# HGRN mixer on one Trainium2 core: decays as products of forget gates built by doubling, one group of small products per head, two weight buffers

## The chip, the cores and the metric

The kernel runs on 1 core of a Trainium2 chip. The metric is device time in microseconds (us), the median of 3 runs. The engines are named as in the profile: PE (TensorE, matrix products), PEld (its weight loads), DVE (VectorE), ACT (ScalarE), POOL (GpSimd) and SP (which issues the loads from memory). All data are float32; the large products are made of float32 numbers split into a high and a low part.

## The reference, cut to what matters

Two residual layers over 512 tokens of width 1024, each a token mixer and an MLP; the first mixer is a gated DeltaNet, the second an HGRN recurrence. The change concerns the second. With a forget gate f per token and channel, lower-bounded by lb, it computes for each of 8 heads (128 channels)

```python
def _hgrn2(y, w_in, lb, gnorm_w, w_out):
    proj = y @ w_in
    q, f, i, gate = jnp.split(proj, 4, axis=-1)
    log_forget = jnp.logaddexp(jnp.log(lb), jnp.log1p(-lb) + jax.nn.log_sigmoid(f))
    k = (1.0 - lb) * jax.nn.sigmoid(-f)
    q = jax.nn.silu(q.astype(f32))
    o = _hgrn2_chunked(heads(q), heads(k), heads(i.astype(f32)), heads(log_forget))
    ...
# S_t = diag(f_t) S_{t-1} + k_t v_t^T (k_t = 1 - f_t), o_t = S_t^T q_t
```

So the output at token t is the sum over earlier tokens j of v_j times the product of q_t, k_j and all forget gates between j and t, summed over channels. The reference works in chunks of 64 with cumulative sums of logarithms; any grouping of the tokens gives the same result.

## The kernel before

Activations stand transposed: channels on the 128 partitions, 512 tokens along a row. Every projection (`project`, L119) takes a weight tile of 256 output columns, loaded by SP into `raw`, split by ACT into its high part `whi` (L116) and by DVE into its low part `wlo` (L117), half a tile per instruction, and makes two blocks of 24 products of 128x512 each (L127, L128, L129). `raw` has two buffers. `whi` and `wlo` have two, and outside the DeltaNet heads a third one (tags `whi3`, `wlo3`), which every third tile takes (L103); the flag `two` switches the third off. Where `stream` (L132) is called with `wide=2`, it starts with two tiles used side by side, channel block by channel block.

`hgrn` (L628) runs over four pairs of heads. `hgrn_in` (L693) projects the next pair's f and q (two tiles) and its values (one tile, 96 products of 128x256, L707 to L709). `hgrn_gates` (L673) projects the output gates of the pair before (one tile). `hgrn_tables` (L713) applies sigmoid and SiLU on ACT and loads their tables. `hgrn_head` (L729) is the mixer of one head, at high priority. The program is written in this order, and a scheduling layer then sets each engine's queue by dependence and priority: the head's small operations are put between projections of the next pair.

In `hgrn_head`, POOL bounds f from below and scales it (L735), ACT takes its logarithm (L736). For pairs of neighbouring tokens, k and q are scaled by exponentials of half the second token's logarithm (L745 to L752) and multiplied in blocks of 32 tokens: `gram32` (L759) makes 16 products of 128x32 by 128x32, four blocks in each of four chunks, in one PSUM tile. DVE scans the logarithms into cumulative sums within 64 tokens (L773). Then for each doubling step s = 2, 4, 8, 16, 32 (`HLEVELS`) DVE subtracts sums at the middle of each block of 2s (L780, L781), ACT takes the exponential (L782), and DVE multiplies the first half with k and the second with q (L783, L784). For s below 32 `gram32` follows, and DVE copies the part that belongs to this step into `ad` under a mask (L787). For s = 32, eight products go to their place by ACT (L793, L796). POOL puts `ad` into the chunk's 128x128 matrix `a` (L798). The exponentials of the whole sums give `qf` and `kg` (L802 to L812), from which come the products across 64 tokens (L816), the transposed `kg` (L824), the states of the chunks (L829, L834, L836) and the output (L841, L843). A product of float32 numbers stands in the trace as two records, the split projections as one.

After the eight heads come the row norm (L188), the output projection (L854) and the MLP.

Of the kernel before, what the change touches and what calls it, by code (L numbers as in the profile page):

```python
# [11 lines left out]
F32 = mybir.dt.float32  # L12
# [3 lines left out]
ALU = mybir.AluOpType  # L16
# [17 lines left out]
class Net:  # L34
# [44 lines left out]
    def after(self, i, prev):  # L79
        self.tc.add_manual_dep(  # L80
            i.ins, prev.ins.name,
            mybir.DependencyInfo(mybir.DependencyClass.NoSync, mybir.DependencyReason.DATA),
            reason="table order")
# [148 lines left out]
    def setup(self, w):  # L232
# [29 lines left out]
        self.lmask = self.mask("lmask", [P, len(LEVELS), B])  # L262
        self.dmask = self.const("dmask", [P, B])
# [364 lines left out]
    def hgrn(self):  # L628
# [17 lines left out]
        self.on = [None] * NH  # L646
        blocks = self.stream(a["hgrn_fq"], self.y, wide=2)
# [10 lines left out]
        for p in range(NH // 2):  # L658
# [11 lines left out]
            pr = nxt  # L670
        self.hgrn_split(range(3, NH))
# [41 lines left out]
    def hgrn_tables(self, pr, gates=()):  # L713
# [13 lines left out]
        self.table("natural_log_exp_and_others")  # L727

    def hgrn_head(self, h, kq, g, vt):  # L729
# [8 lines left out]
        tmp = lambda: self.work("ol", bufs=NH)  # L738
        gram = lambda: self.mix("gr", tag="mb")


        half = tmp()
        hv = half.rearrange("p (a n) -> p a n", a=2)
        gp = g.rearrange("p (n b) -> p n b", b=2)
        self.act(hv[:, 0], gp[:, :, 1], AF.Exp, scale=0.5)  # L745
        self.act(hv[:, 1], gp[:, :, 1], AF.Exp, scale=-0.5)
        dk, dq = tmp(), tmp()
        for dst, src, sg in ((dk, k, 0), (dq, q, 1)):
            d2, s2 = (t.rearrange("p (n b) -> p n b", b=2) for t in (dst, src))
            for b in (0, 1):  # L750
                e = nc.vector
                e.tensor_tensor(out=d2[:, :, b], in0=s2[:, :, b], in1=hv[:, (b + sg) % 2], op=ALU.mult)  # L752
        a = self.work("x" if h % 2 else "e")
        c4 = lambda t: t.rearrange("p (c t) -> p c t", c=NC)
        nc.gpsimd.memset(a, 0.0)
        blk = [slice(b, b + B) for b in range(0, P, B)]
        ad = self.work("wd" if h % 2 else "ud", [P, NC, B])

        def gram32(x, y):  # L759
            pa = self.mix("gr", [P, NC, B], tag="mb")  # L760
            for c in range(NC):
                for b in blk:
                    mm(pa[b, c], lhsT=ck(x, c)[:, b], rhs=ck(y, c)[:, b], start=True, stop=True,  # L763
                       tile_position=(0, b.start))
            return pa

        pa = gram32(dk, dq)
        nc.vector.tensor_tensor(out=ad, in0=pa, in1=self.dmask.unsqueeze(1).to_broadcast([P, NC, B]), op=ALU.mult)


        gc = g
        b64 = lambda t: t.rearrange("p (n s) -> p n s", s=64)
        nc.vector.tensor_tensor_scan(out=gc, data0=self.fresh, data1=g, initial=0.0, op0=ALU.mult, op1=ALU.add)  # L773

        for i, s in enumerate(HLEVELS):
            nb = T // (2 * s)
            v4 = lambda t: t.rearrange("p (n a s) -> p n a s", a=2, s=s)
            e = tmp()
            ref = v4(gc)[:, :, 0, s - 1:s].to_broadcast([P, nb, s])
            nc.vector.tensor_tensor(out=v4(e)[:, :, 0], in0=ref, in1=v4(gc)[:, :, 0], op=ALU.subtract)  # L780
            nc.vector.tensor_tensor(out=v4(e)[:, :, 1], in0=v4(gc)[:, :, 1], in1=ref, op=ALU.subtract)  # L781
            self.act(e, e, AF.Exp)  # L782
            nc.vector.tensor_tensor(out=v4(e)[:, :, 0], in0=v4(e)[:, :, 0], in1=v4(k)[:, :, 0], op=ALU.mult)  # L783
            nc.vector.tensor_tensor(out=v4(e)[:, :, 1], in0=v4(e)[:, :, 1], in1=v4(q)[:, :, 1], op=ALU.mult)  # L784
            if s < B:
                pa = gram32(e, e)
                nc.vector.copy_predicated(out=ad, mask=self.lmask[:, i + 1].unsqueeze(1).to_broadcast([P, NC, B]),  # L787
                                          data=pa)
                continue
            pa = self.mix("gr", [P, NC, B], tag="mb")  # L790
            for c in range(NC):
                for l, r in (blk[0:2], blk[2:4]):
                    mm(pa[l, c], lhsT=ck(e, c)[:, l], rhs=ck(e, c)[:, r], start=True, stop=True,  # L793
                       tile_position=(0, l.start))
            for l, r in (blk[0:2], blk[2:4]):
                nc.scalar.copy(out=c4(a)[l, :, r], in_=pa[l])  # L796
        for b in blk:
            nc.gpsimd.tensor_copy(out=c4(a)[b, :, b], in_=ad[b])  # L798


        qf, kg = tmp(), tmp()
        self.act(qf, gc, AF.Exp)  # L802
        last = self.work("last", [P, 2 * NC], bufs=2)
        egl = self.work("egl", [P, NC], bufs=2)
        nc.vector.tensor_copy(out=last, in_=b64(qf)[:, :, 63])
        lv = last.rearrange("p (c b) -> p c b", b=2)
        nc.vector.tensor_tensor(out=egl, in0=lv[:, :, 0], in1=lv[:, :, 1], op=ALU.mult)
        nc.vector.tensor_tensor(out=qf, in0=qf, in1=q, op=ALU.mult)
        nc.vector.tensor_tensor(out=b64(kg), in0=b64(gc)[:, :, 63:64].to_broadcast([P, 2 * NC, 64]), in1=b64(gc),
                                op=ALU.subtract)  # L810
        self.act(kg, kg, AF.Exp)
        nc.vector.tensor_tensor(out=kg, in0=kg, in1=k, op=ALU.mult)  # L812
        pa = gram()
        for c in range(NC):
            t = c * P
            mm(pa[0:64, t + 64:t + P], lhsT=kg[:, t:t + 64], rhs=qf[:, t + 64:t + P], start=True, stop=True)  # L816
        nc.scalar.copy(out=c4(a)[0:64, :, 64:P], in_=c4(pa)[0:64, :, 64:P])
        for t, half, n in ((kg, slice(0, 64), NC - 1), (qf, slice(64, P), NC)):
            v = c4(t)[:, 0:n, half]
            f = lv[:, 0:n, half.start // 64 ^ 1:(half.start // 64 ^ 1) + 1]  # L820
            nc.vector.tensor_tensor(out=v, in0=v, in1=f.to_broadcast([P, n, 64]), op=ALU.mult)
# [163 lines left out]
def halves(s):  # L985

    p, t = np.arange(P)[:, None] % B, np.arange(B)[None, :]
    return (p // (2 * s) == t // (2 * s)) & (p // s % 2 == 0) & (t // s % 2 == 1)


def turned(m):
    return m.reshape(P // B, B, B).transpose(0, 2, 1).reshape(P, B)


def layout(x, gdn_w_in, gdn_conv, gdn_a_log, gdn_dt_bias, gdn_onorm, gdn_w_out, hgrn_w_in, hgrn_lb_logits,
# [10 lines left out]
    o["lmask"] = np.stack([turned(halves(1))] + [halves(s) for s in LEVELS[1:]], 1).astype(np.float32)  # L1006
    o["dmask"] = ((i[:, None] % B // 2 == i[None, :B] // 2) & (i[:, None] % B <= i[None, :B])).astype(np.float32)
# [33 lines left out]
```

## Time and profile before

| | |
|---|---|
| time, median of 3 runs | 1363.98 us (1363.65 to 1366.46) |
| the profiled execution's own time | 1365.81 us |
| its span in the trace | 1363.7 us |
| granted TensorE clock, mean | 0.996 |
| PE busy | 1338.5 us (98%), 10084 records |
| PEld busy | 1096.9 us (80%) |
| DVE busy | 823.2 us (60%), 1472 instructions |
| ACT busy | 579.3 us (42%), 1061 instructions, 37 table loads |
| POOL busy | 206.1 us (15%), 212 instructions |
| DMA | 121.5 MB, mean 89 GB/s |

The DeltaNet mixer lies at about 40 to 330 us, its output projection and the first MLP reach to about 700, the HGRN mixer fills some 720 to 965, and its output projection and the second MLP the rest. In a timeline row stand the start, the duration, engine, source line, operation, what is written and read, the shape and how many are merged; in brackets how long the engine had been idle and what ended that. Matmuls overlap, so their durations add up to more than their time: what one costs PE is read from the starts of the instructions around it.

### The profile page before, as it was taken

What the parts mean: (1) busy time and instruction counts of PE and PEld (TensorE: products, weight loads), DVE (VectorE), ACT (ScalarE), POOL (GpSimd) and SP (SyncE); (2) the same over time, 40 slices, a digit from 0 to 9 for tenths busy, and PEclk for the clock granted to TensorE, in tenths of its full rate; (3) what the DMA queues carried; (4) which work ended last, traced back from release to release, by engine and by line L of the source; (5) the groups of instructions that cost most, each with busy time, mean ns of one, the idle gap of its engine ahead of it and who ended that gap; (6) DMA issues with size and microseconds to landing.
All of it is one profiled execution on the core that took longest, in us unless ns stands there. A gap on an engine that the chain in (4) does not pass through costs nothing.

```text
span 1363.7 us, 23897 instructions
## 1 busy us (share of the span) xinstructions
PE 1338.5 (98%) x10084; PEld 1096.9 (80%) x10084; DVE 823.2 (60%) x1472; ACT 579.3 (42%) x1061; POOL 206.1 (15%) x212
## 2 busy tenths in 40 slices
PE   7999999999999999999999999999999999999997
PEld 5777777778888888888888788787888888888897
DVE  5886777766844444444483985769774444445453
ACT  5664655444344323132134566476434413314242
POOL 4001011000200120201121123031100021120232
PEclk8999999999999999999999999999999999999999
DMA  6131110222322222232220212121042223232232
GB/s 199 35 122 36 60 63 33 80 78 67 141 103 93 93 93 93 95 114 96 98 93 31 94 64 94 62 94 63 32 154 93 93 93 97 95 115 95 93 134 83
DMA packets 23498, 121.53 MB, mean 89 GB/s; under 512 B 3808, under 2 KB 7008, under 8 KB 9824
## 3 DMA queue, kind: packets, MB, share of 16 engines
q1 hardware_dynamic: 23392, 120.02, 25.3%
q8 instruction: 79, 1.29, 0.4%
q14 instruction: 27, 0.22, 0.1%
HBM read 117.91 MB, written 2.10 MB: 88 GB/s over the span
## 4 chain that ended last, share of the span: by engine, by line
PE 86%; DVE 6%; ACT 5%; issue 2%; DMA 0%; POOL 0%; SPq 0%; POOLq 0%; ACTq 0%; DVEq 0%
PE pj L127 25%; PE pj L128 25%; PE pj L129 24%; ACT L93 1%; PE gr L763 1%; PE pga L478 1%; PE pu L523 1%; ACT whi L116 1%; DVE wlo L117 1%; ACT v L87 1%; PE px L516 1%; PE pw L593 1%; PE pj L709 1%; PE pj L708 1%; PE pj L707 1%
## 5 line engine op out<-in xcount | busy, mean ns | idle before, releaser
L117 DVE TENSOR_TENSOR wlo<-raw,whi 128x1024 fp32r<-128x1024 f32 (+2 forms) x217 | 290.1, 1351 | 167.4 <-ACT whi L116 165.1
L116 ACT CAST whi<-raw 128x1024 fp32r<-128x1024 f32 (+2 forms) x222 | 221.6, 1024 | 398.5 <-PE pj L128 381.8
L127 PE MATMUL pj<-yh,whi 128*128 128x512 f32 x960 | 383.6, 400 | 0.7 <-ACT whi L116 0.7
L129 PE MATMUL pj<-yh,wlo 128*128 128x512 f32 x960 | 382.3, 399 | 0.6 <-DVE wlo L117 0.6
L128 PE MATMUL pj<-yl,whi 128*128 128x512 f32 x960 | 382.1, 398 | 0.0
L127 PEld LDWEIGHTS pj<-yh,whi 128*128 128x128 f32 x960 | 181.7, 189 | 37.4 <-ACT whi L116 1.9
L129 PEld LDWEIGHTS pj<-yh,wlo 128*128 128x128 f32 x960 | 181.7, 189 | 36.6 <-DVE wlo L117 1.0
L128 PEld LDWEIGHTS pj<-yl,whi 128*128 128x128 f32 x960 | 182.0, 190 | 35.4
L128 PE MATMUL pj<-ol,whi 128*128 128x512 f32 x336 | 131.3, 391 | 0.0
L901 DVE TENSOR_TENSOR gate<-pj,rB 128x512 f32<-128x512 f32 x56 | 38.6, 691 | 148.2 <-PE pj L129 148.2
L129 PE MATMUL pj<-oh,wlo 128*128 128x512 f32 x320 | 125.0, 391 | 0.0
L127 PE MATMUL pj<-oh,whi 128*128 128x512 f32 x320 | 124.9, 391 | 0.0
L903 POOL TENSOR_TENSOR kd<-kd,gate 128x512 f32<-128x512 f32 x18 | 23.3, 1292 | 462.2 <-DVE gate L901 458.0
L887 ACT ACTIVATE z<-pj 128x512 f32<-128x512 f32 x64 | 38.0, 594 | 113.6 <-PE pj L129 109.6
L128 PEld LDWEIGHTS pj<-ol,whi 128*128 128x128 f32 x336 | 63.2, 188 | 12.9
L127 PEld LDWEIGHTS pj<-oh,whi 128*128 128x128 f32 x320 | 60.1, 188 | 12.3
L129 PEld LDWEIGHTS pj<-oh,wlo 128*128 128x128 f32 x320 | 60.0, 188 | 12.3
L129 PE MATMUL pj<-kq,wlo 128*128 128x512 f32 (+1 forms) x192 | 68.4, 356 | 0.5 <-DVE wlo L117 0.5
L128 PE MATMUL pj<-kq,whi 128*128 128x512 f32 (+1 forms) x192 | 68.4, 356 | 0.0
L127 PE MATMUL pj<-kq,whi 128*128 128x512 f32 (+1 forms) x192 | 68.0, 356 | 0.0
L167 POOL TENSOR_TENSOR sqacc<-sqacc,z 128x512 f32<-128x512 f32 x25 | 37.3, 1494 | 122.9 <-ACT z L165 118.8
L93 ACT ACT_TABLE_LOAD x37 | 47.5, 1283 | 1.4 <-PEq L1033 0.7
(392 smaller groups left out, 2022.2 us busy)
## 6 DMA issues: line engine op xcount, KB each, us to landing
raw<-down SPq DMA_DIRECT2D x36, 1024.0 KB, 4.8
raw<-up SPq DMA_DIRECT2D x32, 1024.0 KB, 4.8
raw<-gdn_in SPq DMA_DIRECT2D x14, 1024.0 KB, 4.8
raw<-hgrn_fq SPq DMA_DIRECT2D x8, 1024.0 KB, 4.8
raw<-gdn_out SPq DMA_DIRECT2D x4, 1024.0 KB, 5.7
raw<-hgrn_i SPq DMA_DIRECT2D x4, 1024.0 KB, 4.7
raw<-hgrn_gate SPq DMA_DIRECT2D x4, 1024.0 KB, 4.8
raw<-hgrn_out SPq DMA_DIRECT2D x4, 1024.0 KB, 4.8
```

The costliest lines, as they stand in the source:

```text
L87: i = self.nc.scalar.activation(out=out, in_=in_, func=func, **kw)
L93: i = self.nc.scalar.preload_act_table_set(name)
L116: self.nc.scalar.copy(out=hi[:, k], in_=raw[:, k])
L117: eng.tensor_tensor(out=lo[:, k], in0=raw[:, k], in1=hi[:, k].bitcast(F32), op=ALU.subtract)
L127: mm(o, lhsT=hi[:, k, c], rhs=yh, start=(k == 0), stop=False)
L128: mm(o, lhsT=hi[:, k, c], rhs=yl, start=False, stop=False)
L129: mm(o, lhsT=lo[:, k, c], rhs=yh, start=False, stop=(k == NB - 1))
L167: e.tensor_tensor(out=self.sq, in0=self.sq, in1=t, op=ALU.add)
L478: mm(pga[:, c - c2], lhsT=ck(k, c), rhs=kq[:, :, c * P:(c + 1) * P], start=True, stop=True)
L887: nc.scalar.activation(out=z, in_=out, func=AF.Relu)
L901: nc.vector.tensor_tensor(out=t, in0=out, in1=self.r2b, op=ALU.mult)
L903: e.tensor_tensor(out=self.h[c], in0=self.h[c], in1=t, op=ALU.add)
```

## The change

It is in `hgrn_head` and around it.

- The decays are products of forget gates instead of exponentials of sums of logarithms. ACT makes `upto` = f scaled and bounded by lb in one instruction, POOL sets `behind` to one. `upto` holds for each token the product of gates from the start of its block to it, `behind` the product from behind it to its block's end. From blocks of s to blocks of 2s, one DVE product multiplies `behind` of the first halves by the second halves' total, and one `upto` of the second halves by the first halves' total, in place. Before each of these steps one DVE product writes both operands of the step: `behind` times k in the first halves, `upto` times q in the second. `qf` and `kg` are two products at the end. The logarithm, the scan, all exponentials and POOL's bounding and scaling are gone. ACT, not POOL, copies `ad` to its place.
- Step s = 1 has products of its own: k with q (masked to the diagonal) and k with q times f. So there are seven groups per head instead of six: six of 16 products and one of 8. All are issued behind the last DVE product of the chain: the first waits for it (the new argument `kind` of `after`), the others are ordered behind the first. They go to two PSUM tiles and are then copied under masks one after the other.
- `upto` and `behind` (four rows of 512) and `qf` and `kg` (four more) lie in the third weight buffer, so the HGRN stage works with two. `a` is cleared once per buffer instead of once per head. The products across 64 tokens use all 128 columns of `kg`.
- The table of logarithms and exponentials is loaded once behind the heads instead of after each pair. The mask `dmask` and its load are gone, `lmask` has one row more.

The diff, cut to its core:

```diff
-    def after(self, i, prev):
+    def after(self, i, prev, kind=mybir.DependencyClass.NoSync):
...
         self.on = [None] * NH
+        self.two = True
         blocks = self.stream(a["hgrn_fq"], self.y, wide=2)
...
-        self.fresh = self.work("rB", bufs=2)
-        nc.gpsimd.memset(self.fresh, 1.0)
-        nc.gpsimd.memset(self.fresh.rearrange("p (n s) -> p n s", s=64)[:, :, 0:1], 0.0)
+        xa, xb = (self.wp.tile([P, 2, 2, T], F32, tag=t, bufs=1, name=self.name(t)) for t in ("whi3", "wlo3"))
+        self.ba = [xa[:, i] for i in (0, 1)]
+        self.fg = [(xb[:, i, 0], xb[:, i, 1]) for i in (0, 1)]
+        self.hat = [self.work(t) for t in ("e", "x")]
+        for t in self.hat:
+            nc.gpsimd.memset(t, 0.0)
...
+        self.nw_tiles, self.two = 0, False
+        self.table("natural_log_exp_and_others")
         self.hgrn_split(range(3, NH))
...
-        nc.gpsimd.tensor_scalar(out=g, in0=g, scalar1=1e-37, scalar2=self.oml[:, hs], op0=ALU.max, op1=ALU.mult)
-        self.act(g, g, AF.Ln, bias=self.lb[:, hs])
+        tmp = lambda: self.work("ol", bufs=NH)
+        mul = lambda o, x, y: nc.vector.tensor_tensor(out=o, in0=x, in1=y, op=ALU.mult)
+        ba, (qf, kg) = self.ba[h % 2], self.fg[h % 2]
+        behind, upto = ba[:, 0], ba[:, 1]
+        nc.scalar.activation(out=upto, in_=f, func=AF.Identity, scale=self.oml[:, hs], bias=self.lb[:, hs])
         nc.scalar.activation(out=q, in_=q, func=AF.Copy, scale=self.oml[:, hs])
...
+        nc.gpsimd.memset(behind, 1.0)
...
+        qa = tmp()
+        mul(qa, upto, q)
+        parts = [(k, q), (k, qa)]
+        for s in (1,) + HLEVELS:
+            v4 = lambda t: t.rearrange("p (n a s) -> p n a s", a=2, s=s)
+            if s > 1:
+                e = tmp()
+                mul(e.rearrange("p (n a s) -> p n a s", a=2, s=s), halves(ba, s), halves(kq, s))
+                parts.append((e, e))
+            for t, i in ((behind, 0), (upto, 1)):
+                end = v4(upto)[:, :, 1 - i, s - 1:s].to_broadcast([P, T // (2 * s), s])
+                mul(v4(t)[:, :, i], v4(t)[:, :, i], end)
...
+        mul(kg, behind, k)
+        last = mul(qf, upto, q)
...
+        pa = [self.mix("gr", [P, n, NC, B], tag="mb") for n in (4, 3)]
+        lead = None
+        for i, (x, y) in enumerate(parts):
+            o = pa[i // 4][:, i % 4]
+            wide = i == len(parts) - 1
             for c in range(NC):
...
+                for l, r in ((blk[0:2], blk[2:4]) if wide else zip(blk, blk)):
+                    m = mm(o[l, c], lhsT=ck(x, c)[:, l], rhs=ck(y, c)[:, r], start=True, stop=True,
+                           tile_position=(0, l.start))
+                    if lead is None:
+                        lead = m
+                        self.after(m, last, mybir.DependencyClass.Sync)
+                    else:
+                        self.after(m, lead)
...
-            nc.gpsimd.tensor_copy(out=c4(a)[b, :, b], in_=ad[b])
+            nc.scalar.copy(out=c4(a)[b, :, b], in_=ad[b])
...
-            mm(pa[0:64, t + 64:t + P], lhsT=kg[:, t:t + 64], rhs=qf[:, t + 64:t + P], start=True, stop=True)
+            mm(pa[:, t + 64:t + P], lhsT=kg[:, t:t + P], rhs=qf[:, t + 64:t + P], start=True, stop=True)
```

In the program as scheduled, the small products of a head stand elsewhere on PE's queue. Here is the queue of before among the first head's products: `gr` are the small products' PSUM tiles, `ol` their operands, `pj` the projections of the next pair.

```order
L127 MATMUL pj_7061<-yh_6595,whi_7054 128x512
L763 MATMUL gr_7326<-ol_7320 32x32 x16
L128 MATMUL pj_7061<-yl_6596,whi_7054 128x512
L763 MATMUL gr_7350<-ol_7344 32x32 x16
L129 MATMUL pj_7061<-yh_6595,wlo_7055 128x512
L127 MATMUL pj_7061<-yh_6638,whi_7054 128x512
L128 MATMUL pj_7061<-yl_6639,whi_7054 128x512
L129 MATMUL pj_7061<-yh_6638,wlo_7055 128x512
L127 MATMUL pj_7061<-yh_6673,whi_7054 128x512
L128 MATMUL pj_7061<-yl_6674,whi_7054 128x512
L763 MATMUL gr_7374<-ol_7368 32x32 x16
```

After, the same head's products on PE (`wlo_1057_6915` is the third weight buffer, which now holds `kg` and `qf`; L808 are the products across 64 tokens):

```order
L126 MATMUL pj_7087<-yl_6715,whi_7054 128x512
L786 MATMUL gr_7320<-kq_6920 32x32 x16
L786 MATMUL gr_7320<-ol_7289,kq_6920 32x32 x16
L786 MATMUL gr_7320<-ol_7293 32x32 x16
L786 MATMUL gr_7320<-ol_7297 32x32 x16
L786 MATMUL gr_7321<-ol_7301 32x32 x16
L786 MATMUL gr_7321<-ol_7305 32x32 x16
L786 MATMUL gr_7321<-ol_7309 32x32 x8
L808 MATMUL gr_7438<-wlo_1057_6915 128x64 x4
L127 MATMUL pj_7087<-yh_6714,wlo_7055 128x512
```

The 104 products of the head stand together and the products across 64 tokens directly behind them; before, 46 runs hold the 48 groups of the eight heads, now there are 8 runs.

The second place is where the first two tiles of the stage end and the first values are projected. Before, on PE (`whi_6787` is the second tile, `whi_1062_6928` the value tile in the third buffer):

```order
L128 MATMUL pj_6797<-yl_6752,whi_6787 128x512
L129 MATMUL pj_6797<-yh_6751,wlo_6788 128x512
L707 MATMUL pj_6936<-whi_1062_6928,yh_6508 128x256
L708 MATMUL pj_6936<-wlo_1063_6929,yh_6508 128x256
L709 MATMUL pj_6936<-whi_1062_6928,yl_6509 128x256
```

After, at the same place (`whi_6929` and `wlo_6930` are the value tile, now in a buffer that the first tile held before):

```order
L126 MATMUL pj_6795<-yl_6750,whi_6785 128x512
L127 MATMUL pj_6795<-yh_6749,wlo_6786 128x512
L710 MATMUL pj_6937<-whi_6929,yh_6506 128x256
L710 MATMUL pj_6963<-whi_6929,yh_6506 128x256
L710 MATMUL pj_6989<-whi_6929,yh_6506 128x256
L711 MATMUL pj_6937<-wlo_6930,yh_6506 128x256
L712 MATMUL pj_6937<-whi_6929,yl_6507 128x256
```

Three products that need only the high part are drawn forward, ahead of the first that needs the low part. The DeltaNet stage, whose code is the same, is scheduled in a slightly different order as well: among other places, the block of 16 products for its decays (`pab`) stands three projections earlier at the start.

More of the change, by code (lines that the diff above doesn't have):

```diff
@@ L261, in setup @@
         nc.sync.dma_start(out=self.tri, in_=self.a["tri"])
-        self.lmask = self.mask("lmask", [P, len(LEVELS), B])
-        self.dmask = self.const("dmask", [P, B])
+        self.lmask = self.mask("lmask", [P, len(LEVELS) + 1, B])
         self.ident32 = self.const("ident32", [P, B])
@@ L745, in hgrn_head @@
[L745 to L753, printed above, removed]
@@ L771, in hgrn_head @@
[L771 to L796, printed above, removed]
@@ L797, in hgrn_head @@
-        for b in blk:
-            nc.gpsimd.tensor_copy(out=c4(a)[b, :, b], in_=ad[b])
[L801 to L808, printed above, removed]
@@ new lines, in hgrn_head @@
+        nc.vector.tensor_tensor(out=ad, in0=pa[0][:, 0], in1=self.ident32.unsqueeze(1).to_broadcast([P, NC, B]),
+                                op=ALU.mult)
+        for i in range(1, len(parts) - 1):
+            m = (len(LEVELS), 1, 2, 3, 4)[i - 1]
+            nc.vector.copy_predicated(out=ad, mask=self.lmask[:, m].unsqueeze(1).to_broadcast([P, NC, B]),
+                                      data=pa[i // 4][:, i % 4])
+        for l, r in (blk[0:2], blk[2:4]):
+            nc.scalar.copy(out=c4(a)[l, :, r], in_=pa[1][l, 2])
```

43 lines of the change are left out of this document (16 added, 27 removed).

## The prediction

> **What bounds the kernel now.** I read four views in this order: the busy times by stretch, what TensorE waited for, the groups of its instructions, and the timeline around one head. The stretches are 40 to 330 us (the DeltaNet mixer) and 722 to 965 us (the HGRN mixer, nearly the only code that is edited); columns are the stretch, its length, then busy us (instructions) of PE, PEld, DVE, ACT and POOL, the granted clock, DMA share and GB/s:
>
> ```profile
> 40.00:330.00 290.00, 284.36 (x3694) 223.70 (x3692) 218.55 (x555) 158.59 (x434) 30.82 (x57) 1.00 0.20 67
> 722.00:965.00 243.00, 239.89 (x2644) 196.48 (x2643) 174.49 (x390) 147.00 (x240) 49.39 (x52) 1.00 0.21 74
> ```
>
> In the HGRN stretch PE is busy 239.89 of 243.00 us at full clock. DVE has 68 us free there, ACT 96. So work taken from DVE, ACT or POOL is worth nothing by itself; only what shortens PE's own row of work, or its idle 3.11 us, counts. The waits of PE from 725 to 965 us (us in total, times, longest) account for nearly all of that idle time, and each is a small product waiting for its DVE operand:
>
> ```profile
> PE gr L763 <- DVE ol L784: 1.7, 5, 0.5
> PE gr L793 <- DVE ol L784: 0.7, 1, 0.7
> PE gr L763 <- DVE ol L752: 0.3, 1, 0.3
> PE po L843 <- DVE s L834: 0.2, 1, 0.2
> ```
>
> That is 2.9 us; the first three rows make seven waits of 2.7 us, 0.39 us on average.
>
> **The small products: what grouping them saves.** The groups of PE's instructions from 740 to 960 us show how many there are (each product stands as two records, so x32 in a timeline row is 16 products):
>
> ```profile
> L763 PE MATMUL gr<-ol 128*32 128x32 f32 x1024 | 14.6, 198 | 1.7 <-DVE ol L784 1.7
> ...
> L763 PE MATMUL gr<-ol,ol 128*32 128x32 f32 x256 | 3.7, 199 | 0.4 <-DVE ol L752 0.3
> L793 PE MATMUL gr<-ol 128*32 128x32 f32 x128 | 3.6, 198 | 0.7 <-DVE ol L784 0.7
> ```
>
> 1280 records at L763 are 40 groups of 16 products, 128 at L793 are 8 groups of 8: five and one per head. Busy times of matmuls overlap, so I cost a group by starts. One group of each kind stands here among projections:
>
> ```profile
> 759.74 0.39 PE L127 MATMUL pj<-yh,whi 128*128 128x512 f32 x1
> 760.05 0.46 PE L763 MATMUL gr<-ol 128*32 128x32 f32 x32
> 760.44 0.50 PE L128 MATMUL pj<-yl,whi 128*128 128x512 f32 x1
> 760.87 0.45 PE L793 MATMUL gr<-ol 128*32 128x32 f32 x16
> 761.25 0.50 PE L129 MATMUL pj<-yh,wlo 128*128 128x512 f32 x1
> 761.58 0.39 PE L127 MATMUL pj<-yh,whi 128*128 128x512 f32 x1
> ...
> 762.49 0.39 PE L128 MATMUL pj<-yl,whi 128*128 128x512 f32 x1
> ```
>
> Undisturbed, projections start 0.227 us apart (761.58 to 762.49 in four steps). From 759.74 to 761.58 pass 1.84 us with three of them; the two groups cost 1.84 - 0.68 = 1.16, so 0.58 us each. Once two groups stand in a row:
>
> ```profile
> 885.24 0.39 PE L127 MATMUL pj<-yh,whi 128*128 128x512 f32 x1
> 885.56 0.82 PE L763 MATMUL gr<-ol 128*32 128x32 f32 x64
> 886.31 0.50 PE L128 MATMUL pj<-yl,whi 128*128 128x512 f32 x1
> 886.65 0.39 PE L129 MATMUL pj<-yh,wlo 128*128 128x512 f32 x1
> ```
>
> 1.41 us less two projections is 0.95, so the second group costs 0.37: about 0.2 us of an isolated group's price is spent on going from projections to small products and back. The order of before has 46 runs for its 48 groups: 46 x 0.58 + 2 x 0.37 = 27.4 us. After, each head has one run of seven groups (one more than before, since the first doubling step needs its own products): 8 x (0.58 + 6 x 0.37) = 22.4. **Gain 5.0 us**; 0.37 rests on a single pair of groups.
>
> The order of after puts the cross products (L816 before) straight behind that run. Alone they cost:
>
> ```profile
> 763.62 0.39 PE L127 MATMUL pj<-yh,whi 128*128 128x512 f32 x1
> 763.94 0.68 PE L816 MATMUL gr<-ol,ol 128*64 128x64 f32 x8
> 764.55 0.50 PE L128 MATMUL pj<-yl,whi 128*128 128x512 f32 x1
> 764.88 0.39 PE L129 MATMUL pj<-yh,wlo 128*128 128x512 f32 x1
> ```
>
> 1.26 - 0.45 = 0.81 us, of which 0.61 lies between their own start and the next projection's. If the run shares its way in and out with them, 0.2 us a head go: **gain 1.6 us**, at worst 0 (they now use 128 weight columns instead of 64, which no row shows for 64 moving ones). I take 1.6, since they are neighbours in the order without a projection between.
>
> **Waits of PE.** The 2.9 us of waits above end with the separate groups. In their place each head's first product waits for one DVE instruction, the last product of the decay chain; queued behind it on PE's queue are the rest of the run and all projections. Eight waits at the mean of the seven seen, 0.39 us: **3.1 us** back. Ends: 0 (DVE is early) and about 1 us each, 8 us. That the two are near each other shows in the sum from the first head's run to the second's. PE has there 52 projections (11.8 us), 10 of the narrow value projections at 0.11 (rows below; 1.1) and the run with the cross products (0.58 + 6 x 0.37 + 0.61 = 3.4): 16.3 us, and the state's and the output's products besides. What DVE has there is worked out from its issue steps in this profile:
>
> ```profile
> 749.11 1.22 DVE L773 TENSOR_TENSOR_SCAN v<-rB,v 128x512 f32<-128x512 f32 x1
> 750.24 1.20 DVE L117 TENSOR_TENSOR wlo<-raw,whi 128x1024 fp32r<-128x1024 f32 x1
> 751.36 0.29 DVE L768 TENSOR_TENSOR ud<-gr,dmask 128x128 f32<-128x128 f32 x1
> 751.56 0.42 DVE L780 TENSOR_TENSOR ol<-v 128x256 f32<-128x256 f32 x1
> 751.89 0.42 DVE L781 TENSOR_TENSOR ol<-v 128x256 f32<-128x256 f32 x1
> ...
> 760.22 0.69 DVE L809 TENSOR_TENSOR ol<-v 128x512 f32<-128x512 f32 x1
> 760.82 0.30 DVE L787 COPY_PREDICATED ud<-lmask,gr 128x128 f32<-128x128 uint8 x1
> ```
>
> A product over half a head takes a step of 0.33, over a whole head 0.60, a masked step 0.20, the scan 1.13, half a weight split 1.12. The chain after is 12 half products (4.0), 8 whole ones (4.8), six small masked steps (1.2): 10.0 us. Before, 24 half products, the scan, three whole products and five masked steps made 7.9 + 1.1 + 1.8 + 1.0 = 11.8. With one weight split (2.2), two projections' scalings (1.2) and the first head's two cross scalings and three state steps (five instructions of half size or less, under 1.7), DVE has some 15 us between the two runs, and a wait of its own for the first run's products. PE's 16.3 and more just cover it, so I expect waits of tenths of a microsecond. ACT's exponentials and logarithm, POOL's floor-and-scale (L735) and the reloads of tables go; nothing of PE waited for them in the list above, so I cost that at nothing; its cover is the projections queued between a pair's heads.
>
> **Two weight buffers.** A tile lasts PE some 11 us (48 x 0.227), while its split takes ACT 2.1 us and DVE 2.4 (two halves, rows below), so two buffers do in mid-stage. They do not at one place: the stage begins with two tiles used side by side, and the third tile had its own buffer. Now its split starts when the first tile is released. The row for such a release is here, beside the stage's first value projections, with DVE's next rows:
>
> ```profile
> 737.56 1.05 ACT L116 CAST whi<-raw 128x1024 fp32r<-128x1024 f32 x1 [13.50 <-PE pj L128]
> ...
> 738.47 0.69 DVE L699 TENSOR_TENSOR kq<-pj,rB 128x512 f32<-128x512 f32 x1
> 739.08 1.22 DVE L117 TENSOR_TENSOR wlo<-raw,whi 128x1024 fp32r<-128x1024 f32 x1
> ...
> 738.95 0.28 PE L707 MATMUL pj<-whi,yh 128*128 128x256 f32 x1
> 739.06 0.28 PE L708 MATMUL pj<-wlo,yh 128*128 128x256 f32 x1
> ```
>
> The high half is then there in time for 738.95, the low half at 739.08 + 1.22 = 740.30. PE has three narrow products (0.33) that do without it: a new wait of 740.30 - 739.28 = **1.0 us** (ends 0 and 2.5, the latter if the second halves wait too).
>
> **The rest.** The order of the DeltaNet stage changes a little as well: one load of a mask goes, and a block of 16 products stands three projections earlier. PE idles 5.64 us there in all; I count 0, with 1.5 us either way.
>
> **Sum.** -5.0 - 1.6 - 2.9 + 3.1 + 1.0 = -5.4 us. The profiled execution took 1365.81 us (span 1363.7, so 2.1 around it); it would take 1360.4. It lies 1.8 above the median of the timed runs, 1363.98, so I forecast 1358.6.
>
> **Rivals.** Less than 0.2% (2.7 us) cannot be told from no change here.
>
> (a) Waits eat the gain. At 0.9 us a head: -9.5 + 1.0 + 7.2 = -1.3, 1362.7: the same. For it: DVE fills whole stretches while two heads follow each other. Against: the mean of 0.39. Chance 0.18.
>
> (b) Slower, by DVE's one long chain. It needs over 1.4 us a head (-9.5 + 1.0 + 8 x 1.4 = +2.7); at 2 us it is +7.5, 1371.5. The mechanism is seen once: POOL adds squares while DVE works, and PE waits.
>
> ```profile
> 951.56 1.28 POOL L167 TENSOR_TENSOR sqacc<-sqacc,z 128x512 f32<-128x512 f32 x1 [12.16 <-ACT z L165]
> ...
> 951.80 1.32 DVE L781 TENSOR_TENSOR ol<-v 128x256 f32<-128x256 f32 x1
> ...
> 954.91 0.45 PE L793 MATMUL gr<-ol 128*32 128x32 f32 x16 [0.75 <-DVE ol L784]
> ```
>
> The DVE product took 1.32 instead of 0.42 us and ended with POOL's. One such hit of 0.9 in each chain, on top of 0.39, gives 1.3 a head: not quite enough, and L735's work on POOL is gone. Chance 0.07. The Trainium skill ("SBUF — State Buffer", SBUF: two separate sides) states the rule: a DVE operation with two SBUF inputs and a GpSimd operation that reads SBUF lock each other out for a whole instruction. The trace agrees at 951.80; by the rule every product of the new chain is exposed, but the memsets on POOL are not readers.
>
> (c) Slower, because a long run of small products does not keep its rate. If each of the seven groups costs 0.58, a head has 4.06 + 0.61 instead of 3.43 + 0.81: +3.4 for eight, and +3.4 - 2.9 + 3.1 + 1.0 = +4.6, 1368.6. Against: the pair at 885.56. Chance 0.05. The Trainium skill ("TensorE: Matmul & The Clock Gate", Wait — 56ns, not 53.3ns?) gives a floor of about 25 ns from start to start, however small the product. Taken per record, 208 of them would be an estimated 5.2 us a head by that page; 64 records in 0.95 us are 15 ns each, so it can hold only per product.
>
> (d) More than forecast: no waits at the runs, 1363.98 - 9.5 + 1.0 = 1355.5. Chance 0.2, against 0.5 for the forecast. That the grouping isn't there is excluded by the order.
>
> **Range and chances.** Faster is the forecast and (d): 0.70. Same 0.18, slower 0.12. Low end: (d) less 1.5 for the DeltaNet order, 1354.0. High end: waits of 0.9, the cross products' 1.6 not gained, and half of the DeltaNet order's 1.5: -1.3 + 1.6 + 0.8 = +1.1, 1365.1, which holds (a).
>
> **What would show it.** Right: eight runs of 208 small records in PE's timeline, each about 2.6 us, then cross products with 0.6; PE waits at L786 of 2 to 5 us in all; one wait of 1 us at L711 near the stage's start; the stage some 5 us shorter. Wrong: run lengths over 3.5 us; waits at L786 above 1 us each; waits on whi or wlo at other places; or a change outside 722 to 965 us larger than that within.

## The result and the profile after

The changed kernel took 1379.1 us (median of 4 runs, 1377.35 to 1383.52) beside 1364.29 of the kernel before (4 runs, 1363.65 to 1366.46): 1.0111 times as long, interval 1.0084 to 1.0137. The forecast was 1358.6, at most 1365.1: the kernel became slower where faster was forecast. The profiled execution took 1378.38 us, 12.57 more than the one of before.

The two stretches that the prediction began with, in the changed kernel (same columns):

```profile
40.00:330.00 290.00, 284.51 (x3693) 224.76 (x3691) 218.06 (x551) 157.86 (x431) 32.49 (x57) 0.99 0.19 66
722.00:965.00 243.00, 225.83 (x2844) 196.77 (x2844) 166.99 (x332) 112.78 (x192) 12.16 (x12) 0.97 0.20 66
```

In the HGRN stretch PE is now idle for 17.2 us instead of 3.1, and its clock was granted at 0.97 instead of 1.00. To see the whole stage whatever its order, I take from the timelines the time between the first row-sum product of the norm ahead of it (719.1 before, 719.2 after) and that of the next norm (1047.5 and 1059.7): 328.4 us before, 340.6 after. So **12.2 of the 12.57 us are lost in this stage**. What PE waited for there, from 725 to 1065 us:

```profile
PE gr L786 <- issue: 12.8, 6, 2.4
PE gr L786 <- DVE wlo L739: 1.9, 3, 0.9
PE pj L711 <- DVE wlo L115: 0.8, 1, 0.8
PE pj L711 <- issue: 0.7, 1, 0.7
PE pt L816 <- DVE wlo L739: 0.6, 1, 0.6
PE pj L127 <- DVE wlo L115: 0.5, 1, 0.5
PE ps L821 <- ACT ol L818: 0.3, 1, 0.3
```

The waits that the prediction argued about are there in about the forecast size: 1.9 us at L786 with 0.6 and 0.3 at the transposes and states behind it, where 3.1 was forecast, and 0.8 at L711, where 1.0 was. The large row is another: 12.8 us in six pieces at the small products, ended by "issue", that is by no engine and no transfer that this list can name; 0.7 more stands at L711. The timeline has one of them in the middle of the second head's run:

```profile
784.38 0.28 PE L710 MATMUL pj<-whi,yh 128*128 128x256 f32 x1
784.59 0.46 PE L786 MATMUL gr<-kq 128*32 128x32 f32 x32
784.87 0.46 PE L786 MATMUL gr<-ol,kq 128*32 128x32 f32 x30
...
785.17 0.96 PE L786 MATMUL gr<-ol 128*32 128x32 f32 x92
788.03 0.73 PE L786 MATMUL gr<-ol 128*32 128x32 f32 x50 [1.89 <-issue]
788.69 1.10 PE L808 MATMUL gr<-wlo 128*128 128x64 f32 x8
789.60 0.36 PE L711 MATMUL pj<-wlo,yh 128*128 128x256 f32 x1
```

158 records pass in 1.36 us, then PE stands for 1.9 us between two products of one group, and the last 50 follow at the same rate. The run takes 4.1 us; "over 3.5 us" was the prediction's first sign of being wrong.

Behind some of these stops the clock falls. Busy times by stretch, around the first and the sixth head's run:

```profile
764.00:768.00 4.00, 2.18 (x40) 1.89 (x27) 1.91 (x7) 0.53 (x2) 0.00 (x0) 1.00 0.02 4
768.00:771.50 3.50, 3.50 (x13) 2.83 (x11) 2.15 (x5) 3.39 (x9) 0.00 (x0) 0.51 0.00 0
873.90:877.30 3.40, 1.00 (x103) 0.89 (x93) 2.74 (x5) 1.95 (x3) 0.00 (x0) 1.00 0.31 46
877.40:884.10 6.70, 6.70 (x33) 5.95 (x26) 2.08 (x8) 2.43 (x8) 0.00 (x0) 0.50 0.33 139
```

After a stretch in which PE did little, it runs at half clock for 3.4 or 6.8 us. The stage has three such stretches (768.10, 877.33, 945.59), 13.65 us in all; before it had none.

**What the stops have in common.** PE's weight loads, products and semaphore instructions, numbered in order of start, place the stops of the changed kernel so:

```
stop after (us)   length   instruction   modulo 256
102.17            2.27      1729         193    (DeltaNet stage)
764.07            2.01     11969         193    head 1
785.94            2.09     12481         193    head 2
806.71            0.96     13249         193    head 3, behind the run
824.78            2.18     13761         193    head 4
855.00            2.44     14529         193    head 5
874.13            2.59     15041         193    head 6
941.76            2.61     16577         193    head 8
```

A length runs from the start of the last instruction ahead of the stop to the start of the next one, so it is 0.2 to 0.3 us more than the idle time of the list. All stops stand at the same place of a period of 256. Transfers have that period too. The page of the changed kernel lists them by queue:

```profile
q8 instruction: 81, 1.33, 0.4%
```

81 packets of 16 KB for PE's 20,761 instructions, 256 in each. In the stop at 785.94, one such packet runs from 785.68 to 786.61, and PE goes on 1.4 us after it ends. The stage's other stops are alike. In all seven a packet starts 0.8 to 1.3 us after PE enters the block ahead of the stop (784.84 here), takes 0.9 to 1.4 us, and PE goes on 1.3 to 1.6 us after its end. Hence **theory F (fetch)**: PE's instructions come in blocks of 256; entering one block starts the fetch of the next, which in these stops can be used 3.2 to 3.8 us later (784.84 to 788.03 here). A projection is two instructions in 0.227 us, so a block of projections lasts 29 us; small products are 8.6 ns a record with its weight load (1.36 us by 158), so a block of them lasts 1.1 us. A run of 416 instructions drains what is there and then waits. The Trainium skill ("Runtime: NRT & Kernel Launch", Instruction fetch mechanics) also has blocks of 256 instructions, fetched one ahead. It says that the crossing is mostly hidden because instructions are dispatched more slowly than blocks are filled; here it isn't hidden, and the measurement decides.

The trace of before had such a stop, also at instruction 1729. It is among the "5.64 us there in all" that the prediction put aside:

```profile
102.90 0.59 PE L523 MATMUL pu<-ud,xd 32*32 32x32 f32 x44
104.79 0.38 PE L523 MATMUL pu<-ud,xd 32*32 32x32 f32 x20 [1.30 <-issue]
```

At this stop the packet starts late: in the kernel before 2.4 us after PE enters the block ahead of the stop, in the changed kernel 3.4. PE again goes on 1.4 and 1.6 us after the packet's end, so the next block is usable only after 5.1 and 5.9 us. The time from block to block is therefore not fixed; what holds the packet up there stays open.

The rivals: **theory W (data)**, the stops are waits for late DVE products or for PSUM that the profile can't name; **theory C (clock)**, small products in number lower the clock by themselves, and the stops are not what does it.

### The profile page after: what moved, and what is told of

It is laid out like the page before. It is cut to its first block, busy times and chain, and to the rows that moved or that the text cites. A ratio compares the mean times of both kernels' runs of the same rounds, so it can differ in the third digit from the quotient of the medians.

```text
span 1376.6 us, 24205 instructions
## 1 busy us (share of the span) xinstructions
PE 1337.1 (97%) x10340; PEld 1108.8 (81%) x10340; DVE 818.0 (59%) x1416; ACT 548.2 (40%) x1016; POOL 170.7 (12%) x172
## 3 DMA queue, kind: packets, MB, share of 16 engines
q8 instruction: 81, 1.33, 0.4%
## 4 chain that ended last, share of the span: by engine, by line
PE 85%; DVE 8%; ACT 3%; issue 2%; DMA 1%; POOL 0%; SPq 0%; POOLq 0%; ACTq 0%; DVEq 0%
PE pj L126 24%; PE pj L125 24%; PE pj L127 24%; DVE whi L739 1%; DVE ol L739 1%; PE gr L786 1%; DVE wlo L115 1%; PE pga L475 1%; DVE kq L393 1%; PE pw L590 1%; PE pu L520 1%; PE gr L808 1%; PE px L513 1%; ACT whi L114 0%; PE po L602 0%
## 5 line engine op out<-in xcount | busy, mean ns | idle before, releaser
L125 PEld LDWEIGHTS pj<-oh,whi 128*128 128x128 f32 x320 | 60.2, 188 | 12.2
L127 PEld LDWEIGHTS pj<-oh,wlo 128*128 128x128 f32 x320 | 60.0, 188 | 12.2
L739 DVE TENSOR_TENSOR whi<-whi 128x256 f32<-128x256 f32 x96 | 40.5, 423 | 7.7 <-ACT whi L742 5.8
```

What stands on the lines that cost most here:

```text
L125: mm(o, lhsT=hi[:, k, c], rhs=yh, start=(k == 0), stop=False)
L127: mm(o, lhsT=lo[:, k, c], rhs=yh, start=False, stop=(k == NB - 1))
L739: mul = lambda o, x, y: nc.vector.tensor_tensor(out=o, in0=x, in1=y, op=ALU.mult)
```

## Experiments on the stops

Each stands against runs of the kernel before on the same chip; stage lengths are from the profiled executions, measured as above (before 328.4, after 340.6).

**Operands ready early (early).**

```diff
             wide = i == len(parts) - 1
+            x, y = k, q
```

> The changed kernel, but all seven groups of a run read k and q (ready long before), so the decay chain's products are left out of the result; each run's first product still waits for the end of the chain. F: runs of 416 instructions run dry as before: 5 to 8 idle stretches of about 2 us within the runs, 9 to 17 us in all. W: with the operands long there, no idle stretch within a run: 0 to 2 us in all.

1376.02 us in one execution, stage 339.1. PE's waits from 700 us on begin with

```profile
PE gr L787 <- issue: 12.3, 6, 2.3
PE gr L787 <- DVE wlo L739: 1.9, 3, 0.9
```

The stops stay, in the same number and about the same size, each at 193 modulo 256. W is ruled out as far as operands go.

**128 instructions ahead (phase128).**

```diff
             nc.tensor.matmul(warm, lhsT=zeros[:, 0:P], rhs=zeros[:, 0:WARM], start=True, stop=True)
+        for _ in range(32):
+            nc.tensor.matmul(warm[:, 0:16], lhsT=zeros[:, 0:P], rhs=zeros[:, 0:16], start=True, stop=True)
```

> The changed kernel with 32 tiny products (128 instructions) added at the start, while PE waits for its first weights: all later PE instructions move by 128 places in the stream, nothing else moves. F, with 3.3 us from block to block: idle stretches in the HGRN stage of 2.2 us in heads 1, 3 and 7, 0.9 in head 8, 0.7 in head 5, under 0.5 in heads 2, 4 and 6: 9.0 us in all instead of 13.5; the one of 2.1 us at 102 us in the DeltaNet stage goes; 1368 to 1374 by what the clock does. W and C: the same six heads stall at the same products for the same 13 us, within 1 us of 1378.

1371.22 us, 1.0031 times before (1.0019 to 1.0043); stage 334.0. Its waits:

```profile
PE gr L788 <- issue: 6.7, 3, 2.5
PE gr L788 <- DVE wlo L741: 1.9, 3, 0.9
PE pt L818 <- DVE wlo L741: 1.9, 4, 0.7
PE pj L125 <- issue: 1.2, 1, 1.2
```

The three long stops are in heads 1, 3 and 7, as the model had them, again at 193 modulo 256; the DeltaNet stage's is gone. The model's small ones (0.7 and 0.9) did not show, and one of 1.2 stands behind head 6's run instead: 7.9 us in all, 9.0 expected. The second head's run, with the same products and operands, now goes through:

```profile
785.52 0.46 PE L788 MATMUL gr<-kq 128*32 128x32 f32 x32
785.79 0.46 PE L788 MATMUL gr<-ol,kq 128*32 128x32 f32 x30
...
786.10 1.51 PE L788 MATMUL gr<-ol 128*32 128x32 f32 x142
787.54 0.66 PE L810 MATMUL gr<-wlo 128*128 128x64 f32 x4
```

2.0 us from its start to the cross products instead of 4.1. Where a stop falls is set by the place in the instruction stream and not by the products. The kernel is otherwise the same, so data and PSUM (W) are ruled out, and a period in the stream with a 16 KB packet in each stop is what F says.

**Ungrouped (spread).**

```diff
-                    if lead is None:
-                        lead = m
-                        self.after(m, last, mybir.DependencyClass.Sync)
-                    else:
-                        self.after(m, lead)
```

> The changed kernel without the grouping: the small products of each part wait for their own DVE operand alone, and the scheduler spreads them between projections again (56 runs of 8 to 16 products instead of 8 runs of 104). Theory F (fetch): PE's instructions arrive in blocks of 256, and a block can be used about 3.3 us after PE enters the one before it; a run of 104 products is 416 instructions in about 2 us, so PE runs dry. Then here no idle time above 0.6 us between small products that no engine ends, no half-clock stretch between 700 and 1000 us; from the profiled 1378.4: -13.5 (the idle stretches) -6.8 (half of 13.6 us at half clock) +48 x 0.2 (ways in and out of runs) = 1367.7. Theory W (data): the idle stretches are waits for late DVE products or for PSUM; they stay as waits of 10 us or more, 1376 to 1380. Theory C (clock: small products by themselves lower it): idle goes only in part, half-clock stretches in the stage stay.

1371.12 us, 1.0036 times before (1.0022 to 1.005); stage 333.3, with no stop by issue and no half clock in it, though there are as many small products: C is ruled out. The time is 3.4 above F's sum. The stage has 4.0 us of idle time; the changed kernel's has 17.6, and 6.8 go to half clock. Without these, 329.3 stand against 316.2 us, so by this estimate 48 separate runs cost about 0.27 us each instead of F's 0.2.

**Two runs a head (tworuns).** The lead is the product that the rest of a run is ordered behind. A new lead stands at the fifth group; the first run's lead waits for that run's last operand.

```diff
+            if i == 4:
+                lead = None
...
-                        self.after(m, last, mybir.DependencyClass.Sync)
+                        self.after(m, (muls[4], last)[i // 4], mybir.DependencyClass.Sync)
```

> The changed kernel with each head's run cut in two, 64 products and 40, with 26 to 54 other products between. F: a run of 64 is 256 instructions, one block, and nearly every block now holds ten or more projections; at most one or two idle stretches, under 2 us in all, and no half-clock stretch in the stage. 1378.4 - 13.5 - 6.8 + 8 x 0.2 + about 1 = 1360.7, faster than both kernels. W: the products still wait for the same DVE results: 1375 to 1380. C: as many small products in each run of 3.4 us, so half-clock stretches stay: about 1368 (13.5 less idle, the rest stays).

1363.46 us, 0.9983 times before (0.9971 to 0.9995); stage 327.3. The stretch of the stage, and its first waits:

```profile
722.00:965.00 243.00, 235.09 (x2900) 202.22 (x2899) 172.39 (x344) 119.41 (x199) 13.69 (x12) 1.00 0.22 75
```

```profile
PE gr L790 <- DVE wlo L739: 4.3, 6, 1.2
PE ps L825 <- ACT ol L822: 2.6, 8, 0.4
```

The stops and the half clock are gone from the stage with one more lead a head: 13.3 us of it. The time is 2.8 us above F's 1360.7; the two rows above are 6.9 us of waits for DVE and ACT, where the changed kernel had 2.8. Its runs also give the price of grouping undisturbed:

```profile
769.01 0.40 PE L125 MATMUL pj<-yh,whi 128*128 128x512 f32 x1
769.34 0.46 PE L790 MATMUL gr<-kq 128*32 128x32 f32 x32
769.62 0.46 PE L790 MATMUL gr<-ol,kq 128*32 128x32 f32 x30
...
769.92 0.71 PE L790 MATMUL gr<-ol 128*32 128x32 f32 x62
770.57 0.50 PE L126 MATMUL pj<-yl,whi 128*128 128x512 f32 x1
```

1.56 us less one projection is 1.33 for four groups: 0.58 and three times 0.25, where the prediction had 0.37.

**Narrow cross products (narrow),** in the kernel with two runs.

```diff
-            mm(pa[:, t + 64:t + P], lhsT=kg[:, t:t + P], rhs=qf[:, t + 64:t + P], start=True, stop=True)
+            mm(pa[0:64, t + 64:t + P], lhsT=kg[:, t:t + 64], rhs=qf[:, t + 64:t + P], start=True, stop=True)
```

> The two-run kernel with the cross products as before: 64 weight columns and 64 result rows instead of 128 and 128 (only those 64 rows are read). The wide ones take 0.91 us from their start to the next projection, the narrow ones before took 0.61: if the width is the cause, 8 x 0.3 = 2.4 us less than the two-run kernel, 1361.1. If their price is only the way in and out, no change: 1363.5.

1362.0 us, 0.9978 times before (0.9968 to 0.9987). The stage goes from 327.3 to 324.9: the 2.4 expected. Each of the eight groups of cross products takes 0.61 us up to the next projection, in the two-run kernel 0.91 or 0.92. In whole times the step (0.0005) is within the intervals; up to the HGRN norm the two profiled executions already differ by 1.5 us.

**112 instructions ahead of that (narrow112),** 28 tiny products as in phase128.

> The kernel with two runs and narrow cross products, and 28 tiny products (112 instructions) at the start, while PE waits for weights. F: with 3.3 us from block to block no block boundary is then late by more than 0.1 us, also not the one at 101 us in the DeltaNet stage (2.0 us idle, and 3.4 us at half clock behind it): 2.0 + 1.7 = 3.7 us less than without the 28 products, about 1357.4, and no half-clock stretch between 40 and 1350 us. Rival: the place in the stream is nothing to PE, and it is as fast as without them, 1361, with the idle time still there.

1360.33 us, 0.996 times before (0.9948 to 0.9973); it and narrow112pool (below) are the fastest kernels here. No stop by issue and no half clock between 40 and 1349 us. From the last product of the decay inputs (`pab`) to the norm ahead of the HGRN it takes 679.26 us, narrow 683.72: 4.46 less, 3.7 expected. The profiled executions differ by 4.6 us (1357.79 and 1362.39). In whole times the gain is not shown: the five executions lie at 1357.7 (two) and 1360.4 (three), the medians differ by 1.7, and the intervals of the two ratios overlap. The longer executions may lose at the start, where narrow112pool, with the same 28 products, ends `pab` 2.9 us later; no trace shows one of them.

**A lead that waits for less (earlier), and that with 120 instructions ahead (earlier120).**

```diff
-                        self.after(m, (muls[4], last)[i // 4], mybir.DependencyClass.Sync)
+                        self.after(m, (muls[4], muls[7])[i // 4], mybir.DependencyClass.Sync)
```

> The two-run kernel with narrow cross products, and the second run's first product waiting for the last operand of its own run instead of for the very end of the decay chain, which comes four DVE instructions later. If the 4.3 us of waits for DVE in the two-run kernel are waits for that end: 2 to 3 us of them go, less 8 x 0.2 that the cross products then stand apart; 1360 to 1361. If DVE is late by more than that anyhow, they stay: 1362 to 1363.

> The kernel whose second run starts at its own last operand (1365.0), with 30 tiny products (120 instructions) at the start. F: its trace has block boundaries late by 2.6 us at 794 us and by 1.7 at 100 us, the latter with 3.4 us at half clock; by the model of 3.3 us a block no boundary is late at this place of the stream: 2.6 + 1.7 + 1.7 = 6.0 us less, about 1359. Rival (nothing hangs on the place in the stream): 1365.

1364.97 us, 1.0009 (0.9997 to 1.0021), and 1363.79, 0.9988 (0.998 to 0.9997); stages 328.9 and 327.5. The first one's wait for DVE hardly shrinks (3.9 us, now for the run's own last operand), so it was not the chain's end alone that PE waited for: a miss, and slower than either forecast. The move in the stream removes the stop of 2.6 us and the DeltaNet stage's, as F says, but only 1.2 us of the 6.0 appear in the median: at the new place PE waits 4.6 us for DVE, and the start is 4.7 us later.

**The same move elsewhere (narrowmid).** 56 tiny products of one record ahead of the first products of `gdn_decay` instead of 28 at the start.

> The kernel with two runs and narrow cross products, and 56 tiny products of one record each (112 instructions) among the first products of the DeltaNet stage instead of 28 of two records at the start, where they took 9 us of a busy start. F: the same move of 112 places in the stream, so no late block boundary and no half-clock stretch between 40 and 1350 us: the stretch from the end of the first products to the DeltaNet stage's last output product 287 us instead of 291.7, at a price of 1 us or less for the tiny products: 1362.0 - 4.0 + 1.0 = 1359. Rival (nothing hangs on the place in the stream): 1362 to 1363.

1363.69 us, 0.9991 (0.9981 to 1.0), runs from 1360.87 to 1366.37. The profiled execution is the fastest, 1360.87. It has no stop by issue over 0.3 us and no half clock between 40 and 1348 us. The stretch forecast at 287 us takes 291.7, but holds 17 projections more than in narrow (an estimated 3.9 us); up to the norm ahead of the HGRN the time from the last `pab` falls from 683.72 to 682.00, with a wait of 1.7 us at one transpose of L622 on the way. The median shows no gain over narrow: a miss. How much of a removed stop is kept depends on what is late next; that was not followed further.

## Experiments on the other terms

**Two weight buffers in the kernel before (beforetwo), and with the diagonal copies on ACT (beforetwoact).**

```diff
+        self.two = True
         blocks = self.stream(a["hgrn_fq"], self.y, wide=2)
...
-            nc.gpsimd.tensor_copy(out=c4(a)[b, :, b], in_=ad[b])
+            nc.scalar.copy(out=c4(a)[b, :, b], in_=ad[b])
```

(The last two lines in beforetwoact only. At the end of the stage both kernels set the flag back, as the changed kernel does.)

> The kernel before with nothing changed but the weight buffers of the HGRN stage: two pairs in turn instead of three. If the second buffer pair costs what the trace of the changed kernel shows (one wait of 0.7 to 0.8 us at the third tile's low half), the time is 0.5 to 1.5 us above before, hardly to be told from it. If two buffers are a main cause of the loss, 5 us or more above before.

1375.34 us, 1.0085 (1.0071 to 1.0099), 10.5 above before on this chip, which is the second case of the expectation; stage 337.2, so 8.8 longer. The wait at the third tile is 0.7 us as expected, so most of the loss is elsewhere. In its timeline, POOL's copies for the first head and the output products that read them:

```profile
760.23 8.08 POOL L800 COPY e<-ud 32x128 f32<-32x128 f32 x4 [15.88 <-DVE ud L789]
768.36 0.49 PE L843 MATMUL po<-e,uw 128*128 128x128 f32 x2 [3.85 <-POOL e L800]
```

The first of the four copies takes 7.09 us, while DVE works on without a pause; the other three take 0.28 to 0.29, and the median of the run is 0.36. Half clock follows (3.4 us).

> The kernel before with two pairs of weight buffers in the HGRN stage, and with the copies of the masked diagonal blocks on ACT instead of POOL, as the changed kernel has them. With two buffers alone it took 1375.3: one POOL copy that otherwise takes 0.3 us took 7 us while DVE ran product after product, and PE waited 3.9 us for it at the output products and then ran 3.4 us at half clock. If POOL beside DVE is the cause, ACT copies in 0.3 us and some 6 us or more go: 1366 to 1369, and what is left over before is the price of the two buffers. If the buffers themselves cost it: 1374 to 1376.

1370.19 us, 1.0034 (1.0021 to 1.0047); stage 334.3. About 5 us go with POOL's copies by the medians, less than expected, and 2.9 of the stage by the profiled executions. 5.9 of the stage stay, with waits of 0.2 to 0.9 us for DVE and ACT at many lines and 3.4 us of half clock. So in the old kernel two buffers cost more than the one wait. What they cost in the changed one can't be separated this way, since the third pair's place is in use for the products; there the trace shows 0.8, and tworuns, narrow and narrow112 are below before with two buffers.

**The copies back on POOL (narrow112pool):** the reverse of that edit, in narrow112.

> The best kernel so far (two runs a head, narrow cross products, 112 instructions ahead; 1360.3) with the diagonal copies back on POOL. If a POOL copy is held while DVE multiplies, then DVE's longer chain holds it in several heads: output products wait 1 to 4 us each, 5 to 15 us in all, 1365 to 1375. If moving the copies was worth nothing, as the prediction had it: 1360 to 1361.

1359.8 us, 0.9957 (0.9943 to 0.9971); stage 323.9 beside 324.5: the move was worth nothing here. A copy takes up to 1.37 us, and PE waits 2.2 us for them in five pieces, but 2.3 instead of 4.7 for DVE at the small products and 0.2 instead of 2.2 for ACT.

## Why the prediction was wrong, by its steps

The stage's 12.2 us, with the rows measured since: grouping 8 x (0.58 + 6 x 0.25) - 27.4 = -10.8; cross products 8 x 0.3 = +2.4; waits for DVE and ACT 2.8 - 2.9 = -0.1; the third tile +0.8; stops by issue 12.8 + 0.7 = +13.5; half clock, half of 13.65, +6.8. Sum +12.6. The stage as a whole closes in the same way: its idle time grew from 3.6 to 17.6 us, half clock cost 6.8, so the rest of PE's row became 8.6 us shorter (-10.8 + 2.4 = -8.4 by the rows).

- **The step that failed is "what grouping them saves": a run of seven groups at 0.58 + 6 x 0.37, "gain 5.0 us".** It carried a pair of groups (64 records, 128 instructions) over to 208 records and 416 instructions, as though only PE's own rate mattered. The rate is even better (0.25 a group, so the gain without stops is 10.8), but PE is not fed at it. phase128, tworuns and spread show that the stops come from the run's length in instructions and its place in the stream.
- **A term that the sum did not have: the clock.** It was read as 1.00 and left there. The stops of some 2 us among small products brought 13.65 us at half clock.
- **"The order of the DeltaNet stage ... I count 0":** right, since the norm ahead of the HGRN begins at 719.14 us before and at 719.16 after. But the row that mattered lay there, 1.30 us ended by issue within small products. It was counted as idle time of another stage, and what it was was not asked. (The changed kernel's stop there is 2.08 us, with 3.4 us at half clock behind it; what made up for that was not followed.)
- **Cross products, "gain 1.6 us, at worst 0":** wrong in sign. They cost 0.91 us up to the next projection instead of 0.61 (788.69 to 789.60 above), and narrow shows that the 128 weight columns are the cause, the very thing that "no row shows".
- **Waits at the runs, 3.1 us forecast:** 2.8 with those of the transposes and the states, three of them at the runs instead of eight. Right in kind; the size may be partly luck, since PE's stops leave DVE time to catch up (not tested by itself): with fewer stops these waits are 4.5 us in phase128, and without the long ones 6.9 in tworuns, which has two leads a head. Rivals (a) and (b) did not come. (In the rows shown for (b) the DVE product ends at 953.12, 0.28 us behind POOL's and not with it.)
- **Two weight buffers, +1.0:** 0.8 at the place named. Right for this kernel's trace, wrong as a general price (beforetwo).
- **ACT's and POOL's work at nothing:** PE waits for none of POOL's work in the changed kernel's list, and 0.3 us for ACT's. Of the moved work only the copies were tested by themselves, in a later kernel (narrow112pool), where the move was worth nothing; the exponentials and the scaling were not. The prediction does not name the copies.
- **Rival (c), a long run that doesn't keep its rate:** nearest in outcome, not in mechanism. It slowed each group; in fact the groups run fast and the run stops. The floor of about 25 ns that it cited from the Trainium skill ("TensorE: Matmul & The Clock Gate", Wait — 56ns, not 53.3ns?) does not hold for these products: 16 of them take 0.28 us (769.34 to 769.62), 17.5 ns each.

## What to carry to other kernels

Count a run of small products in instructions, not only in time, and ask how long the last 256 of them took: two groups in a row were cheap here, a run of 416 instructions was not, and cutting it in two gave more than all the waits argued about. Idle time that the profile ends with "issue" in the middle of one group is a question to answer before anything is made longer there, above all when its place in the stream repeats. Instructions added far ahead can move such a stop: 128 of them made this stage 6.6 us shorter (phase128). What a row does not show (a width, a length) has to be bounded in both directions, also when the neighbour looks alike.

## What the hardware showed that was not expected

- PE's instructions arrive in packets of 16 KB. In the HGRN stage's stops a block is usable 3.2 to 3.8 us after PE enters the one before it, so 256 instructions in less time cost the difference, 2.0 to 2.6 us in the long ones. Where the packet starts late it is more (5.9 us in the DeltaNet stage, 5.1 in earlier's stop at 794 us). 128 instructions more at the start moved or removed every stop.
- The clock fell to half for 3.41 or 6.83 us after only 1.4 to 2.5 us of idle time in the 3.413 us just ahead (14 falls between 40 and 1340 us in all traces together). On a grid of 3.413 us through the falls, each window with over 1.9 us of idle time was followed by one, those with 1.4 to 1.9 us only in part. The stretches of the changed kernel start 109.23 and 68.26 us apart, 32 and 20 times 3.413. The Trainium skill ("TensorE: Matmul & The Clock Gate", Part 1: The HAM clock gate (the "warmup" mystery)) has a free-running window of 3413 ns, which agrees; a whole idle window, which it names as the cause, was not needed here. Not every stop brings it (none after heads 2, 4 and 5); what decides among the shorter ones stays open.
- A POOL copy of 0.3 us took 7.09 us beside DVE operations without a pause (beforetwo). It cost time because the output products waited for it (3.85 us); the kernel before had one of 3.6 us that nobody waited for.
